# Four groups of instructions moved in the issue order of a fused hybrid decoder layer: sample scores, first query span, first gates, sample softmax

## The chip, the cores and the metric

One Trainium2 chip, one core. The metric is the device time of one execution in microseconds (us). Engines: TensorE (PE; its weight loads are PEld), VectorE (DVE), ScalarE (ACT), GpSimd (POOL), and SyncE (SP), which here issues the DMA transfers. Each engine works through its own queue of instructions in the order in which the program issues them, and waits where an instruction's data or buffer is not ready.

## The reference

One step of a decoder layer (sequence 4096, model width 1024, float32). A combined input projection gives q, k, v, two gates and the LRU input. Half of the heads' width is dilated window attention, the other half a gated linear recurrence; both are gated, concatenated, projected, added to the input and normalised.

```python
def _layer(x_p, x_s, ck, cv, sc, sh, w_in, ...):
    q, k, v, ga, xl, gl = _project(x_p, w_in)
    # 8 heads x 64; patterns (window, dilation) (128,1), (512,4), (2048,16)
    y_att = _merge([_dilated_prompt(qh, kh, vh, d) for _, d in DIL_PATTERNS])
    # causal conv of width 4, then two block-diagonal gates and a linear scan
    h_lru, conv_p, h_p = _lru_branch(xl, 0, 0, conv_w, conv_b, w_ra, b_ra, w_ri, b_ri, lru_lambda)
    y_p = _finish(x_p, y_att, ga, h_lru, gl, w_out, ln_g, ln_b)
    # the same for 8 x 4 sample tokens, against caches of 2048 keys and values
    ...

def _finish(x, y_att, g_att, h_lru, g_lru, w_out, ln_g, ln_b):
    mixed = concatenate([y_att * silu(g_att), h_lru * silu(g_lru)], axis=-1)
    z = ALPHA * x + einsum('bte,ed->btd', mixed, w_out)
    return layer_norm(z) * ln_g + ln_b
```

The prompt is one sequence of 4096 tokens; the sample is 8 sequences of 4 new tokens, each with 2048 cached keys and values. Sample scores are products of the new queries with cached keys, summed over 64 channels.

## The kernel before

Every matrix product is made of three matmuls: each operand is split into a high and a low part, and high x high, high x low and low x high are summed. The order of issue is written out by hand: nothing is reordered behind the program's back, so what the code issues first stands first in its engine's queue.

**Projections (0 to 591 us).** Eight tiles of 512 tokens. For tiles 1 to 6 the program issues four Q groups, four K groups (`qk_group`; 24 matmuls of 128x512 each, L316 to L318) and the value groups (`v_groups`; 96 matmuls, L190). ScalarE and VectorE copy and split each Q or K group (L204, L205), and SyncE stores it (L194). While TensorE works on the values of tile t, `next_chunk` prepares the eight X chunks of tile t+1: VectorE transposes (L111), ScalarE rounds (L114), VectorE takes the difference (L115), SyncE stores a copy for later (L82). `evac_v` then copies four value blocks to tiles `vt` (L210) and stores them (L212). Behind each Q or K group stands one `decode_step`: it issues what the dictionary `decode` holds for that group of the sample scores. A piece is a load of keys (`dec_load`, L366 or L370: 1 MB, or 256 KB for the pattern of dilation 1), a multiply by the queries (`dec_mul`, L375), a sum (`dec_sum`, L380) and a store (`dec_save`, L383). Twelve pieces start at every second group:

```python
g = 2 * n
for d, f in ((0, dec_load), (1, dec_mul), (2, dec_sum), (3, dec_save)):
    decode.setdefault(int(g + d), []).append((f, b, p))
```

Key tiles lie in a pool of two; the small keys lie in the ring of three tiles `vt` that the value copies use too. In the last tile `kp_group` (four transposes, L335, of keys for the output, and their store, L339), `each` (gate weights and the X chunks of a later filler, L123 and L75), `load_K` (L439) and `load_Q` (L446) stand around the groups: attention's first K and the four spans of its first Q.

**Attention (592 to 1457).** Eight units of scores, softmax and values, with projections of the output gate as filler between them (L707 to L712); `vload` loads the values. The first matmul (L562) needs K and the first Q span.

**LRU (1430 to 1900).** 16 tiles of 256 tokens, each in two halves p (called pairs here). Per tile: projection `xl` (`xl_mm`, L140 to L144, 48 matmuls per pair), convolution on VectorE (L958), split of u to `uh` (ScalarE L966, VectorE L967), gates (`gate_mms`, 12 matmuls per pair, L921 to L923; `gate_act`; `gate_vec`), scan, output gate. The order is a list of functions sorted by tick, 18 ticks per tile; `t0` and `t0x` give tile 0 ticks of its own. X chunks come from DRAM (L75); `gated_load`, `gated_mul`, `gated_store` (L1149, L1153, L1157) stand between them.

**Out projection (1888 to 2333).** 32 blocks of 128 tokens (48 matmuls of 128x512, L1341). Per block, VectorE adds the residual (L1395), takes the statistics (L1399, L1401), and scales (L1406, L1408, L1421), and splits the mixed input of a later block (L1330). In between run the remaining sample pieces: multiplies (L1494) and sums (L1498) of keys, two softmax passes `soft1` to `soft6` (mask add L1501, transposes L1507 and L1509, maximum and exponential L1515 to L1519, normalising L1523 to L1526, transposes L1531, copies to `Z` L1536), and sums over values on TensorE (L1551). The order is the dictionary `plan`, sorted by tick; a block is 8 ticks. `soft_at` holds the ticks of the two softmax passes, `v_step` the spacing of the value pieces behind each.

Of the kernel before, what the change touches and what calls it, by code (L numbers as in the profile page):

```python
# [30 lines left out]
class Kern:  # L31
# [125 lines left out]
    def phase1(self, xs_ctx):  # L157
# [9 lines left out]
        n_t = SEQ // 512  # L167
# [216 lines left out]

        for n, (b, p) in enumerate([(b, p) for b in range(self.early) for p in (2, 0, 1)]):
            g = 2 * n
            for d, f in ((0, dec_load), (1, dec_mul), (2, dec_sum), (3, dec_save)):
                decode.setdefault(int(g + d), []).append((f, b, p))
            if p == 2:
                decode.setdefault(g, []).append((row_q, b))  # L390
        order = dec_mul, row_q, dec_sum, dec_save, dec_load
        tick = [0]
# [6 lines left out]
        def qk_groups(t, j, kp, each=None):  # L399
            for m in range(4):  # L400
                qk_group(t, j, m)
                decode_step()
                if kp >= n_t // 2:
                    kp_group(kp, m)
                if each:
                    each()
# [20 lines left out]
        self.KT = self.S[1].rearrange("p (g h n) -> p g h n", g=8, h=2)  # L427
        for g in (0, 2):
            self.load_K(0, g, 2)
        qk_groups(n_t - 1, 0, n_t - 1, each)  # L430
        self.QT = self.S[0].rearrange("p (g h s n) -> p g h s n", g=4, h=2, s=2)
        for nb in range(4):
            self.load_Q(0, 0, nb)
        ctx.close()

    def load_K(self, c, g, n):
# [6 lines left out]
    def load_Q(self, c, st, nb):  # L443
        for p in range(2):
            for h in range(2):
                self.nc.sync.dma_start(  # L446
                    out=self.QT.bitcast(F32)[p * 64:(p + 1) * 64, nb, h],
                    in_=dap(self.qd, (c * 128 + h * 64) * SEQ + st * ST + nb * SPAN,
                            [[SEQ, 64], [DA * SEQ, 2], [1, SPAN]]))


    def phase2(self):
# [19 lines left out]
        KT, QT, Wg, load_K, load_Q = self.KT, self.QT, self.Wg, self.load_K, self.load_Q  # L472
# [329 lines left out]
        def vload(i):  # L802
            x = steps[i]
            if x.b:
                return
            g = x.st * 4 + x.a
            if x.unit.i == 6 and x.a == 0 and x.pat:
                f = (load_V16, load_V4, load_V1)[x.pat]
                f(x.c, g - 1)
                return defer(5, f, x.c, g)  # L810
            if x.pat == 0:
                if x.st:
                    load_V16(x.c, 0, x.a)
                load_V16(x.c, x.st, x.a)
            elif x.pat == 1:
                load_V4(x.c, g)
            else:
                load_V1(x.c, g)

        vload(0)  # L820
        vload(4)
        feed(self.f0[0])
        N, staged, split = len(steps), 0, 0
        for i in range(N + 26):
# [39 lines left out]
            if i < N and x.b == 3 and (x.pat == 1 and x.a or x.pat == 0 and x.a == 3):  # L864
                nb = x.a if x.pat else 0
# [21 lines left out]
    def phase3(self):  # L887
# [14 lines left out]
        T, n_t = 256, SEQ // 256  # L902
# [320 lines left out]
        for i, (f, g, a) in enumerate(early):  # L1223
            t, b = self.e0 + i // len(self.e1), i % len(self.e1)
# [12 lines left out]
        for t in range(n_t):  # L1237
            for tick, i, f, a in plan:
                if f is x_next and t + 1 == n_t:
                    continue  # L1240
                if t == 0 and f is gl_mm:
                    tick = self.t0[0] + a[0]
                if t == 0 and f is x_next:
                    tick = self.t0x[0] + self.t0x[1] * a[0]
                if t == 0 and a == (1,) and f in (gate_mms, gate_act):
                    tick = self.t0[1 + (f is gate_act)]
                ticks.setdefault(t * period + tick, []).append((i, t, f, a))
        for g in sorted(ticks):
            for i, t, f, a in sorted(ticks[g], key=lambda v: (v[1], v[0])):
# [427 lines left out]
@with_exitstack  # L1677
def tile_hymba_dilated_attn_rglru(ctx, tc, ins, outs):
    k = Kern(ctx, tc, ins, outs)
    k.pr = 0.2, 5.5, 7.0  # L1680
    k.p2 = 6, 9, 5, 1, 1, 3, 4, 3, 7, 11, 12, 16, 20, 24, 24, 24, 24, 17, 381, 387, 3.95
    k.kl, k.lag, k.f0, k.wl, k.fill_rate = k.p2[:7], k.p2[7:13], k.p2[13:18], k.p2[18:20] + (2,), (k.p2[20],) * 8
    k.t0x = 1.5, 1.5, (1,) * 8, (1, 1, 0, 1, 1, 0, 1, 1)
    k.t0 = -9.0, 22.2, 23.0
    k.ev = 0, 1, 0, 0
    k.p4 = 6.55, 12.0, 13.5, 14.1, 18.2, 9.0, 2.0, 6.5
    k.ls = 356, 358, 360, 364, 366, 368, 370, 372, 374, 376
    k.nx = lambda nc, t, c: nc.gpsimd if t == 0 and c % 2 else None
    k.s0 = lambda nc, i: nc.gpsimd if i < 9 and i % 2 else None
    k.soft = 0.49, 2.0, 5.0, 5.5, 9.5, 11.0, 12.75, 4.77, 7.0  # L1690
    k.p3 = 0, 4.0, 3.75, 4.5, 7.4, 8.2, 9.4, 11.8, 12.0, 17.0, 12.2, 13.0, 16.0, 18.5, 25.5, 20.55, 22.2, 28.5, 30.25, 33.0, 31.5, 34.75
    k.svb, k.we, k.wo0, k.wo1, k.wo2 = 4, (lambda nc, j, c: nc.vector), 6.0, 1.4, 4.4
    k.xe, k.le, k.ll = (lambda nc: nc.gpsimd), (lambda nc: nc.gpsimd), 5
    k.e0, k.e1, k.e2, k.smp = 4, (2,), (9,), (5, 14)
    k.early, k.k_start, k.k_step, k.soft_at, k.v_step = 4, 10.0, 22.0, (14.0, 114.0), (24.0, 22.0)
    xs = k.xs_ctx = ExitStack()
    k.phase1(xs)
    k.open_late(xs)
    k.phase2()
    k.phase3()  # L1700
    k.phase4()
    xs.close()
# [28 lines left out]
```

## Time and profile before

| | us |
|---|---|
| median of 3 runs (lowest to highest) | 2335.94 (2334.12 to 2345.07) |
| the profiled execution, its own time | 2335.18 |
| its span | 2333.5 |
| TensorE busy (share of the span) | 2193.2 (94%) |
| VectorE busy | 1424.5 (61%) |
| ScalarE busy | 1093.0 (47%) |
| GpSimd busy | 529.9 (23%) |
| mean granted TensorE clock | 0.97 of full speed |

The span goes from the first to the last instruction; the 1.7 us between it and the time lie around it. The shares are means over stages with different limits. Where an engine stands still, the profile names what ended the wait. The granted clock is given in tenths of full speed; a window that shows 0.50 ran at the lower of two levels.

### The profile page before, as it was taken

The page shows a single profiled execution, that of the slowest core. Times are in us where ns is not written, and L with a number is a line of the kernel's source. Part 1 is how long each engine was busy: PE and PEld are TensorE (multiplying, and loading weights), DVE is VectorE, ACT ScalarE, POOL GpSimd, SP SyncE. Part 2 cuts the span into 40 slices and gives each one's busy share as a digit, 9 for nine tenths or more (in the row PEclk, how much of TensorE's full clock was granted, in tenths as well). Part 3 has the DMA queues.
Part 4 walks back from the last instruction along what each step waited for, and adds up shares of the span by engine and source line. Part 5 has one row for each costly group of instructions (what it writes and reads, how often), then busy time and mean ns, then how long its engine had stood idle before and what let it go on. Part 6 is the DMA issues. An engine that isn't in the chain of part 4 may idle for free.

```text
span 2333.5 us, 42473 instructions
## 1 busy us (share of the span) xinstructions
PE 2193.2 (94%) x15274; PEld 1891.7 (81%) x15274; DVE 1424.5 (61%) x3544; ACT 1093.0 (47%) x2819; POOL 529.9 (23%) x499
## 2 busy tenths in 40 slices
PE   6999999999799989989998997899999988999998
PEld 5887778888688889978988886899999965777776
DVE  4454443332267677766765765677878778865465
ACT  3211112222267657766766673666777742212121
POOL 1000000000247465656837576000000000000000
PEclk9999999999899999999999998999999998999999
DMA  6867666555966888788798665545545656755541
GB/s 176 256 215 224 220 220 211 185 205 187 263 157 165 188 202 190 199 212 199 194 209 204 170 175 125 183 152 167 163 154 181 195 205 239 263 183 191 189 144 59
DMA packets 325058, 444.57 MB, mean 191 GB/s; under 512 B 60405, under 2 KB 195573, under 8 KB 319729
## 3 DMA queue, kind: packets, MB, share of 16 engines
q1 hardware_dynamic: 322128, 432.94, 63.4%
q0 software_dynamic: 2720, 8.92, 1.1%
q8 instruction: 122, 2.00, 0.4%
q14 instruction: 88, 0.71, 0.1%
HBM read 305.99 MB, written 135.80 MB: 189 GB/s over the span
## 4 chain that ended last, share of the span: by engine, by line
PE 69%; DMA 13%; DVE 5%; POOL 5%; SPq 4%; issue 3%; ACT 2%; ACTq 0%; POOLq 0%; DVEq 0%
PE po L1341 15%; PE o L598 6%; PE pp L190 6%; PE pt L582 6%; DMA dk<-in_cache_k_dram 3%; PE s L562 3%; PE s L563 3%; PE pg L1019 2%; PE pg L1021 2%; PE pg L1020 2%; PE pp L316 2%; PE pp L317 2%; PE pp L318 2%; PE xl L144 2%; PE xl L140 2%
## 5 line engine op out<-in xcount | busy, mean ns | idle before, releaser
L512 POOL CAST qg<-S 128x512 fp32r<-128x512 f32 x256 | 277.0, 1105 | 655.7 <-DMA S<-qd 500.0
L1341 PE MATMUL po<-S,mx 128*128 128x512 f32 x1536 | 371.9, 402 | 10.4 <-DVE xr L1395 7.1
L1341 PEld LDWEIGHTS po<-S,mx 128*128 128x128 f32 x1536 | 290.3, 191 | 95.8 <-issue 17.3
L573 ACT ACTIVATE sm<-sm,st 128x256 f32<-128x256 f32 (+1 forms) x512 | 251.8, 493 | 181.9 <-DVE st L569 134.2
L569 DVE CUSTOM_DVE_ANT_0 sm<-s,mask 128x256 f32<-128x256 f32 (+1 forms) x768 | 269.5, 389 | 83.4 <-PE s L563 72.7
L586 DVE COPY pts<-pt 128x512 f32<-128x512 f32 x228 | 157.0, 689 | 147.4 <-PE pt L582 145.1
L582 PE MATMUL pt<-ident,sm 128*128 128x128 f32 x1368 | 227.6, 285 | 0.1
L598 PE MATMUL o<-pts,v 128*64 128x128 f32 x2736 | 197.5, 285 | 6.6 <-DMA v<-vd 5.2
L562 PE MATMUL s<-S,qg 128*128 128x256 f32 x512 | 160.1, 333 | 37.0 <-POOL qg L512 24.5
L190 PE MATMUL pp<-S,xh 128*128 128x512 f32 x768 | 179.2, 393 | 6.5 <-ACT S L128 5.3
L316 PE MATMUL pp<-xh,S 128*128 128x512 f32 x448 | 179.6, 401 | 4.0 <-ACT xh L114 3.5
L582 PEld LDWEIGHTS pt<-ident,sm 128*128 128x128 f32 x1368 | 153.9, 142 | 34.3 <-ACT sm L573 17.2
L317 PE MATMUL pp<-xh,S 128*128 128x512 f32 x448 | 178.7, 399 | 1.7 <-DVE xh L115 1.7
L598 PEld LDWEIGHTS o<-pts,v 128*64 128x64 f32 x2736 | 149.3, 139 | 34.3 <-DMA v<-vd 5.7
L318 PE MATMUL pp<-xh,S 128*128 128x512 f32 x448 | 177.0, 395 | 0.0
L190 PEld LDWEIGHTS pp<-S,xh 128*128 128x128 f32 x768 | 145.5, 190 | 38.6 <-ACT S L128 6.2
L707 PE MATMUL f<-xh,S 128*128 128x256 f32 x512 | 147.8, 289 | 3.4 <-DMA xh<-xtd 3.4
L140 PE MATMUL xl<-xh,S 128*128 128x256 f32 x512 | 146.3, 286 | 4.0 <-DMA xh<-xtd 2.6
L573 ACT ACTIVATE sm<-sm,ac 128x128 f32<-128x128 f32 (+1 forms) x256 | 114.4, 448 | 75.1 <-DVE ac L569 73.5
L205 DVE TENSOR_TENSOR stg<-pp,stg 128x512 fp32r<-128x512 f32 x56 | 50.9, 912 | 159.2 <-ACT stg L204 159.0
L144 PE MATMUL xl<-xh,S 128*128 128x256 f32 x512 | 146.2, 286 | 1.7 <-POOL S L129 0.8
L712 PE MATMUL f<-xh,S 128*128 128x256 f32 x512 | 147.3, 288 | 0.0
(289 smaller groups left out, 5150.9 us busy)
## 6 DMA issues: line engine op xcount, KB each, us to landing
xh<-xtd SPq DMA_DIRECT2D x256, 256.0 KB
S<-qd SPq DMA_DIRECT2D x128, 256.0 KB
xtd<-xh SPq DMA_DIRECT2D x56, 512.0 KB
gb<-wd SPq DMA_DIRECT2D x64, 384.0 KB
v<-vd SPq DMA_DIRECT2D x264, 64.0 KB
S<-kd SPq DMA_DIRECT2D x64, 256.0 KB
xr<-in_x_prompt_dram SPq DMA_DIRECT2D x32, 512.0 KB
arena<-in_cache_v_dram SPq DMA_DIRECT2D x16, 1024.0 KB
```

What stands on the lines that cost most here:

```text
L140: nc.tensor.matmul(out, wh, xh, start=(c == 0), stop=False)
L190: nc.tensor.matmul(p, l, m, start=(c == 0 and a + b == 0), stop=(c == 7 and (a, b) == ((1, 0) if j < 2 else (0, 1))))
L316: nc.tensor.matmul(ps, wh, xh, start=(c == 0), stop=False)
L317: nc.tensor.matmul(ps, wh, xl, start=False, stop=False)
L318: nc.tensor.matmul(ps, wl, xh, start=False, stop=(c == 7))
L512: nc.gpsimd.tensor_copy(o, q.bitcast(F32))
L562: nc.tensor.matmul(s[:, h], q_ap(x, h, 0), k, start=True, stop=False)
L569: nc.vector.tensor_tensor_reduce(x.sm[:, h, o], s[:, h, i], self.mask[:, x.pat, o], -0.125, 3e38, ALU.add, ALU.min, x.stat[:, h, 0:1])
L573: nc.scalar.activation(x.sm[:, h, o], x.sm[:, h, o], AF.Exp, bias=x.stat[:, h, 0:1], scale=-1.0, accum_out=x.stat[:, h, 1:2])
L582: nc.tensor.transpose(p[:, h, kb], x.sm[:, h, kb * 128:(kb + 1) * 128], self.ident)
L598: nc.tensor.matmul(o[h * 64:(h + 1) * 64, x.b * 128:(x.b + 1) * 128], v[:, h * 64:(h + 1) * 64], x.pt[:, h, kb], start=(kb == kbs[0]), sto ...
L1341: self.nc.tensor.matmul(ps[j], l, self.Wo[j][c][:, s], start=(c == 0 and s == 0 and l is mh), stop=(c == 7 and l is ml))
```

## The change

Four edits, all to the order of issue; no instruction is added or removed. Sample pieces in the projections: multiply, sum and store come one group later than before, two, three and four groups behind the load. The last tile's loop is written out, so that the first Q span's load is issued right behind the store of the last Q group, and the other three spans between the two value loads of attention. Tile 0's gates get ticks of their own for both pairs. The first softmax pass moves from tick 14 to 26, the second from 114 to 116, with 22 ticks between value pieces in the first pass in place of 24.

```diff
@@ -384,7 +384,7 @@
 
         for n, (b, p) in enumerate([(b, p) for b in range(self.early) for p in (2, 0, 1)]):
             g = 2 * n
-            for d, f in ((0, dec_load), (1, dec_mul), (2, dec_sum), (3, dec_save)):
+            for d, f in ((0, dec_load), (2, dec_mul), (3, dec_sum), (4, dec_save)):
                 decode.setdefault(int(g + d), []).append((f, b, p))
             if p == 2:
                 decode.setdefault(g, []).append((row_q, b))
@@ -427,10 +427,13 @@
         self.KT = self.S[1].rearrange("p (g h n) -> p g h n", g=8, h=2)
         for g in (0, 2):
             self.load_K(0, g, 2)
-        qk_groups(n_t - 1, 0, n_t - 1, each)
         self.QT = self.S[0].rearrange("p (g h s n) -> p g h s n", g=4, h=2, s=2)
-        for nb in range(4):
-            self.load_Q(0, 0, nb)
+        for m in range(4):
+            qk_group(n_t - 1, 0, m)
+            if m == 3:
+                self.load_Q(0, 0, 0)
+            kp_group(n_t - 1, m)
+            each()
         ctx.close()
 
     def load_K(self, c, g, n):
@@ -818,6 +821,8 @@
                 load_V1(x.c, g)
 
         vload(0)
+        for nb in range(1, 4):
+            load_Q(0, 0, nb)
         vload(4)
         feed(self.f0[0])
         N, staged, split = len(steps), 0, 0
@@ -1242,8 +1247,8 @@
                     tick = self.t0[0] + a[0]
                 if t == 0 and f is x_next:
                     tick = self.t0x[0] + self.t0x[1] * a[0]
-                if t == 0 and a == (1,) and f in (gate_mms, gate_act):
-                    tick = self.t0[1 + (f is gate_act)]
+                if t == 0 and f in (gate_mms, gate_act, gate_vec):
+                    tick = self.t0[1 + a[0]][(gate_mms, gate_act, gate_vec).index(f)]
                 ticks.setdefault(t * period + tick, []).append((i, t, f, a))
         for g in sorted(ticks):
             for i, t, f, a in sorted(ticks[g], key=lambda v: (v[1], v[0])):
@@ -1681,7 +1686,7 @@
     k.p2 = 6, 9, 5, 1, 1, 3, 4, 3, 7, 11, 12, 16, 20, 24, 24, 24, 24, 17, 381, 387, 3.95
     k.kl, k.lag, k.f0, k.wl, k.fill_rate = k.p2[:7], k.p2[7:13], k.p2[13:18], k.p2[18:20] + (2,), (k.p2[20],) * 8
     k.t0x = 1.5, 1.5, (1,) * 8, (1, 1, 0, 1, 1, 0, 1, 1)
-    k.t0 = -9.0, 22.2, 23.0
+    k.t0 = -9.0, (18.5, 18.6, 19.5), (24.5, 24.6, 25.5)
     k.ev = 0, 1, 0, 0
     k.p4 = 6.55, 12.0, 13.5, 14.1, 18.2, 9.0, 2.0, 6.5
     k.ls = 356, 358, 360, 364, 366, 368, 370, 372, 374, 376
@@ -1692,7 +1697,7 @@
     k.svb, k.we, k.wo0, k.wo1, k.wo2 = 4, (lambda nc, j, c: nc.vector), 6.0, 1.4, 4.4
     k.xe, k.le, k.ll = (lambda nc: nc.gpsimd), (lambda nc: nc.gpsimd), 5
     k.e0, k.e1, k.e2, k.smp = 4, (2,), (9,), (5, 14)
-    k.early, k.k_start, k.k_step, k.soft_at, k.v_step = 4, 10.0, 22.0, (14.0, 114.0), (24.0, 22.0)
+    k.early, k.k_start, k.k_step, k.soft_at, k.v_step = 4, 10.0, 22.0, (26.0, 116.0), (22.0, 22.0)
     xs = k.xs_ctx = ExitStack()
     k.phase1(xs)
     k.open_late(xs)
```

VectorE at the boundary between tiles 1 and 2, where the cutting of tile 2's X begins (L111, L115), as a piece of the difference (`dk` are key tiles, `stg` a copied Q or K group, `sc` scores, `vt` values):

```order
 L205 TENSOR_TENSOR stg<-pp,stg 128x32x16
 L380 TENSOR_REDUCE sc<-dk 128x32
-L205 TENSOR_TENSOR stg<-pp,stg 128x32x16
-L375 TENSOR_TENSOR dk<-dk_1302,qb 128x2048
 L111 STREAM_TRANSPOSE raw<-X 128x512
 L115 TENSOR_TENSOR xh<-raw,xh 128x2x256
```

```order
 L115 TENSOR_TENSOR xh<-raw,xh 128x2x256
 L210 COPY vt<-pp 128x512 x2
+L205 TENSOR_TENSOR stg<-pp,stg 128x512
+L375 TENSOR_TENSOR dk<-dk_1300,qb 128x2048
 L205 TENSOR_TENSOR stg<-pp,stg 128x512
 L380 TENSOR_REDUCE sc<-dk 128x32
```

The last multiply that stood ahead of the cutting now stands behind the copies of the values and one Q group; a sum stands ahead of the cutting. The other two such boundaries change alike.

TensorE at the start of the LRU stage, before: the last projection of tile 0 (`xl_16493`), the gates of tile 0, pair 0 (`z`), the first projection of tile 1 (`xl_16615`):

```order
L144 MATMUL xl_16493<-xh_15946,S2_79 128x256
L921 MATMUL z_16584<-uh_16555,S0_77 128x256
...
L923 MATMUL z_16591<-uh_16555,S0_77 128x256
L140 MATMUL xl_16615<-xh_16485,S2_79 128x256
L142 MATMUL xl_16615<-xh_16485,S2_79 128x256
```

The same place in the changed kernel; the first projection of tile 1 is `xl_16586` there, its second `xl_16686`:

```order
L144 MATMUL xl_16493<-xh_15946,S2_79 128x256
L140 MATMUL xl_16586<-xh_16485,S2_79 128x256
...
L144 MATMUL xl_16586<-xh_16582,S2_79 128x256
L926 MATMUL z_16639<-uh_16555,S0_77 128x256
...
L928 MATMUL z_16646<-uh_16555,S0_77 128x256
L140 MATMUL xl_16686<-xh_16485,S2_79 128x256
```

The 12 gate matmuls moved behind the 48 projection matmuls. Those of pair 1 keep their place.

VectorE in the out projection, before: from the mask add (L1501) to the softmax (L1516 on) stand the residual sum of block 1 and what belongs to it (`xr`, `bs`, `mv`: residual, statistics; `mx`: the split mixed input; `SC`, `arena`: sample scores and keys):

```order
L1421 TENSOR_TENSOR xr<-xr,lnb 128x1024
L1501 TENSOR_TENSOR SC_22083<-SC_22083,m_22121 128x128
L1395 SCALAR_TENSOR_TENSOR xr<-xr,po 128x512 x2
L1399 BN_STATS bs<-xr 128x6 x2
L1401 BN_AGGR mv<-bs 128x2
L1498 TENSOR_REDUCE SC_22083<-arena 128x32
L1330 SCALAR_TENSOR_TENSOR mx<-A,mx 128x256 x4
L1494 TENSOR_TENSOR arena<-arena,qb 128x2048
L1516 TENSOR_TENSOR dP<-ds,mn 128x32
```

The changed kernel: the mask add is L1506, the softmax L1521 on, the residual sums L1400:

```order
L1335 SCALAR_TENSOR_TENSOR mx<-B,mx 128x256 x4
L1506 TENSOR_TENSOR SC_22083<-SC_22083,m_22121 128x128
L1411 RECIPROCAL mv<-mv 128x1
L1413 SCALAR_TENSOR_TENSOR xr<-xr,mv,lng 128x1024
L1426 TENSOR_TENSOR xr<-xr,lnb 128x1024
L1400 SCALAR_TENSOR_TENSOR xr<-xr,po 128x512 x2
L1404 BN_STATS bs<-xr 128x6 x2
L1406 BN_AGGR mv<-bs 128x2
L1521 TENSOR_TENSOR dP<-ds,mn 128x32
```

The mask add now stands behind the residual sum of block 2, three key sums and two mix splits further down. On TensorE block 3 has come ahead of the score transposes, and block 4 ahead of the softmax's transposes.

## Rows read from the trace of the kernel before

A row of a stretch gives its limits, its length, the busy us and (x) instructions of PE, PEld, DVE, ACT and POOL, the granted clock, the mean busy share of the DMA engines and GB/s.

**Rows 1.** the page's shares: each engine's busy us, share of the span, instructions.

```profile
PE 2193.2 (94%) x15274; PEld 1891.7 (81%) x15274; DVE 1424.5 (61%) x3544; ACT 1093.0 (47%) x2819; POOL 529.9 (23%) x499
```

**Rows 2.** chain of waits, value groups of tiles 4 and 5: start us, us, engine, output, line.

```profile
366.86 21.76 PE pp L190 x96
434.04 21.76 PE pp L190 x96
```

**Rows 3.** timeline of TensorE, projections: start us, us, engine, line, operation, output<-input, count.

```profile
154.83 18.75 PE L190 MATMUL pp<-S,xh 128*128 128x512 f32 x82
...
227.72 13.99 PE L190 MATMUL pp<-S,xh 128*128 128x512 f32 x61
...
299.76 16.48 PE L190 MATMUL pp<-S,xh 128*128 128x512 f32 x72
...
567.84 0.60 PE L335 MATMUL pp<-ident,kf 128*128 128x128 f32 x4
568.19 0.48 PE L316 MATMUL pp<-xh,S 128*128 128x512 f32 x1
```

**Rows 4.** timeline of VectorE, projections [idle before <-releaser]; then groups, 150 to 345 us.

```profile
164.51 0.70 DVE L111 STREAM_TRANSPOSE raw<-X 128x512 f32<-128x512 f32 x1
...
235.19 2.29 DVE L375 TENSOR_TENSOR dk<-dk,qb 128x2048 f32<-128x2048 f32 x1 [3.41 <-DMA dk<-in_cache_k_dram]
...
310.48 0.70 DVE L111 STREAM_TRANSPOSE raw<-X 128x512 f32<-128x512 f32 x1
...
369.12 0.70 DVE L111 STREAM_TRANSPOSE raw<-X 128x512 f32<-128x512 f32 x1
...
L380 DVE TENSOR_REDUCE sc<-dk 128x32 f32<-128x2048 f32 x10 | 22.8, 2280 | 0.0
```

**Rows 5.** timeline of ScalarE behind the value groups of tile 1.

```profile
196.49 0.59 ACT L210 COPY vt<-pp 128x512 f32<-128x512 f32 x1 [15.66 <-DMA vd<-vt]
```

**Rows 6.** timeline of TensorE, start of attention; then one stretch of all engines.

```profile
606.30 0.55 PE L562 MATMUL s<-S,S 128*128 128x256 f32 x1 [11.31 <-DMA S<-qd]
625.58 0.35 PE L707 MATMUL f<-xh,S 128*128 128x256 f32 x1 [3.35 <-DMA xh<-xtd]
...
605.00:610.00 5.00, 3.40 (x14) 3.17 (x15) 0.51 (x4) 0.88 (x4) 2.27 (x3) 0.50 1.07 226
```

**Rows 7.** timeline of TensorE at the start of the LRU stage, and a stretch behind it.

```profile
1462.48 0.58 PE L922 MATMUL z<-uh,S 128*128 128x256 f32 x1 [5.75 <-DVE uh L967]
1471.21 0.38 PE L140 MATMUL xl<-xh,S 128*128 128x256 f32 x1 [0.29 <-DMA xh<-xtd]
...
1480.00:1875.00 395.00, 395.00 (x3237) 388.90 (x3237) 306.08 (x604) 291.33 (x540) 0.00 (x0) 1.00 0.52 164
```

**Rows 8.** timeline of TensorE in the out projection, blocks 2 to 4.

```profile
1909.79 13.03 PE L1341 MATMUL po<-S,mx 128*128 128x512 f32 x48 [6.57 <-DVE xr L1395]
...
1935.93 0.87 PE L1531 MATMUL dt<-ident,dP 128*128 128x128 f32 x3 [11.71 <-DVE dP L1526]
...
1936.66 13.16 PE L1341 MATMUL po<-S,mx 128*128 128x512 f32 x48
...
1951.70 11.51 PE L1341 MATMUL po<-S,mx 128*128 128x512 f32 x48
```

**Rows 9.** timeline of VectorE in the out projection.

```profile
1922.93 1.28 DVE L1395 SCALAR_TENSOR_TENSOR xr<-xr,po 128x512 f32<-128x512 f32 x2
...
1931.26 0.18 DVE L1516 TENSOR_TENSOR dP<-ds,mn 128x32 f32<-128x32 f32 x1
...
1935.70 0.16 DVE L1406 RECIPROCAL mv<-mv 128x1 f32<-128x1 f32 x1
...
1944.15 2.26 DVE L1498 TENSOR_REDUCE SC<-arena 128x32 f32<-128x2048 f32 x1
...
1947.68 0.14 DVE L1406 RECIPROCAL mv<-mv 128x1 f32<-128x1 f32 x1
```

**Rows 10.** a stretch of the out projection, columns as in the window of rows 6.

```profile
1910.00:1950.00 40.00, 28.25 (x115) 22.09 (x119) 35.63 (x61) 11.39 (x22) 0.00 (x0) 0.79 0.76 279
```

## Prediction

> **What bounds the kernel now.** I read the shares of the engines first: TensorE is busy 94% of the span [rows 1], so the time is TensorE's work plus the stretches in which it stands still or runs slowly. Then I read where it stands still near what the change moves, stage by stage.
>
> In the projections, the four value groups of a tile are 96 matmuls and 21.76 us when nothing stops them [rows 2], 0.2267 us each, so the 288 matmuls of a tile cost at least 65.3 us. The value groups of tiles 1, 2 and 3 end at 173.58, 241.71 and 316.24 (start plus duration) [rows 3], those of tiles 4 and 5 at 388.62 and 455.80 [rows 2]. From end to end the tiles 2 to 5 last 68.1, 74.5, 72.4 and 67.2 us. Tile 5 also holds four groups of four transposes, each 0.35 us from its first to what follows [rows 3], so an undisturbed tile is 67.2 - 1.4 = 65.8. Tiles 2, 3 and 4 lose 2.3, 8.7 and 6.6 us, together 17.6. (Against 65.3 it is 19.1, against 67.2 it is 13.4: the bounds.)
>
> VectorE shows the cause. It must cut and split a tile's X while TensorE works on the values of the tile before. In front of that stands a multiply of a sample piece that waits for its keys: 3.41 us, then 2.29 us of work, to about 237.4 [rows 4]. Counted from the start of the value groups (their end less 21.76: 151.8, 219.9, 294.5) the cutting begins 12.7, 17.5 and 16.0 us late (164.51, 237.4, 310.48), and the tile behind loses 2.3, 8.7 and 6.6. Per us of lateness that is 1.3 us, and nothing is lost up to some 11 us. Tile 4, which has no sample piece there, begins at 369.12 [rows 4], 2.3 us late, and tile 5 loses nothing.
>
> At the hand-over to attention TensorE waits 11.31 us for the Q load and later 3.35 us for an X chunk, while the DMA engines are full (share 1.07, 226 GB/s) and the granted clock is 0.50 [rows 6]. At the start of the LRU stage it waits for the first converted u (last step 5.75 us), and then for X chunks to 1471.21; from 1480 to 1875 it never stops [rows 7]. In the out projection it waits 6.57 us on the first residual sum and 11.71 us on the softmax [rows 8].
>
> **The change part by part**, against the profiled execution, 2335.18 us.
>
> *Sample pieces.* The same loads, multiplies and sums are issued, multiply and sum one group later. At these three boundaries a sum then stands ahead of the cutting, not the multiply that waits. Its operand was multiplied two groups' evacuations before, so it waits for nothing and takes 2.28 us [rows 4]. It follows the last K evacuation, as the cutting in tile 4 does at +2.3, so cutting begins at about 2.3 + 2.2 = +4.5 us, 6.5 us inside the 11 that cost nothing. The displaced multiply now runs behind the value evacuation, where VectorE has nothing else. A load that is still waited for 3.41 us after one group of 5.44 needs some 9 us; two groups give it 10.9. Two prices remain. A small key tile is held for one group longer, in the ring of three that the value copies also use; already ScalarE waits 15.66 us there for a value store to land [rows 5], and it costs TensorE nothing as long as free PSUM banks last (four groups of 5.44 us). And any multiply may still be late for its load, where only sample work stands behind it. I take the whole 17.6 less 0.6 for these: **-17.0**. Bounds: -18, when even the half-clock tail goes, and -12, which is the low loss of 13.4 less 1.4 for one delayed group.
>
> *Q span.* Two 256 KB transfers (a k_prompt store and an X chunk) no longer stand ahead of the first Q span: 0.5 MB at 226 GB/s is 2.2 us, that much earlier could the 11.31 us wait end. But the DMA engines are full, the bytes ahead of the X chunk that is waited for next, at 625.58, are unchanged, and what attention gains before that is lost to a longer wait there. I take **-0.5**; bounds -2.2 and +1 (the first values come behind one Q span, and three spans behind them).
>
> *First gates.* Only the 12 gate matmuls of tile 0, pair 0 change their place on TensorE; pair 1 keeps its own although its numbers are new, and no other engine's order changes. Before, they ran behind the wait for u and ahead of tile 1's first projection, which then waited for X chunks to 1471.21. Now that projection starts at once and waits for the same chunks, which land no earlier: they are queued behind transfers that wait on GpSimd's and the gates' data, not on TensorE. So the projection ends where it did, and the gates, which were covered by its waits, come behind: 12 x 0.122 (395.00 / 3237) = **+1.5**. Behind it TensorE is full to 1875, so it passes through to the end. Bounds: 0, when the chunks come earlier, and +4, when the projection also runs longer at the half clock (12 of its matmuls cost 0.21 there for 0.12).
>
> *Softmax.* All its steps stay and move 12 ticks (the second set 2). Before, the mask add stood just ahead of the residual sums at 1922.93, TensorE did the score transposes, and block 3 waited 11.71 us for VectorE's 4.4 us of softmax (1931.26 to 1935.70) behind six other pieces of work [rows 8, 9]. Now block 3 goes first: it may start at about 1924 (behind two residual sums) and end near 1935.5 (11.5 us). But the mask add has moved behind norms, sums, mix split and multiply of block 1 and 2. VectorE does from 1922.93 to 1947.68 all of that plus the softmax, 4.44, and the weight copies, 1.2 [rows 9]: 24.75 - 5.6 = 19.1 us. The mask add so comes at about 1942 (1922.93 + 19.1), TensorE waits 6.6 us there, block 4 runs from 1943.6 to about 1956.5 with its start at the half clock (48 matmuls took 13.03 and 13.16 behind waits, 11.51 without [rows 8]), and behind it the order puts a norm's end, a residual sum with its statistics, the softmax, two multiplies, a mix split and a scaling, 18.7 us by the same steps, ahead of the weight copies' end, near 1960.7, so the first value matmuls wait 3 us more. Block 5 then starts near 1962.7, or 1964.1 with a second start at the half clock; before, it started at 1964.2 (1951.70 + 11.51, and 8 value matmuls). VectorE is busy 35.63 of 40 us there [rows 10]: the order says who waits, not how much work stands in front. I take **0**; bounds -13 (the wait of 11.71 and its 1.5 us at the half clock really go) and +5 (two more waits, each with such a tail).
>
> TensorE's clock speaks against this part. Behind waits of 6.57 and 11.71 us the rows show 1.5 and 1.7 us more for 48 matmuls. The Trainium skill (TensorE: Matmul & The Clock Gate, section "HAM oscillation — how this bites in real kernels") says that a loop that pauses for data in each pass goes back to the half clock again and again and pays for the return each time. By that, three waits in place of two would cost one return more and the sum would be -14.5; whether a wait of 3 us does it, no row of this stage shows.
>
> Sum: -17.0 - 0.5 + 1.5 + 0 = **-16.0**, 2319.2, rounded to 2319.5. The profiled execution stands 0.8 us under the median of the runs shown (2335.94), so no correction is made. A measurement of this kernel can tell about 0.5%, 11.7 us, from no change: faster means below 2324.3.
>
> **The rivals.**
> - *The softmax wait goes too.* For it: block 3 no longer stands behind the softmax, and VectorE has idle time (4.4 us in 40). Against it: the 19.1 us of work in front. If VectorE gets through it by the end of block 3, about 12 us more are won: 2307.5.
> - *The tile waits go only in part.* For it: the multiply two places ahead of the cutting still waits for keys, and a load of 9 us has under 2 us to spare. If loads take some 20 us now, that multiply, the last copies and the sum come late together and cutting begins at some +13.7; by 1.3 us per us behind +11 each boundary keeps 3.5 us, the tiles gain 7 instead of 17, and with +1 from the rest the time is 2329. It decides from 6.5 us of lateness on.
> - *Slower: the value copies block.* One ring of three tiles serves small key tiles and value copies. With a key tile held across the value evacuation, both copying engines wait for a store to land. The groups behind then fill the PSUM banks, four at the first boundary and five at the others (21.8 and 27.2 us). Stores now let ScalarE go at 196.49, 22.9 us after the value groups end. If they land 33 us after that end, TensorE waits 33 - 21.8 = 11.2 and twice 5.8, 22.8 us, and the time is 2319.2 + 22.8 = 2342. It decides from about 22 us on at the first boundary; I expect VectorE's release near 13 us, when the first of the four stores has landed.
> - *The move does nothing.* Excluded for part 1, whose order differs at all three boundaries; it is so for pair 1 of the gates, and that is in the sum.
>
> **How the numbers follow.** Forecast 0.62, with its own range 2313 to 2327 from the bounds of its terms (-12 to -18 for the tiles, -2.2 to +4 beside them). Softmax gained 0.14; tile waits in part 0.16; slower 0.04; 0.04 spread over other mishaps on both sides. The range takes in the first two rivals' centres and leaves out the slower one and the tails: 2307 to 2330. Faster by over 0.5%: 0.14 and nearly all of 0.62 (0.56), 0.70; within 0.5%: the rest of the forecast, the third case and half of the spread, 0.26; slower 0.04.
>
> **What would show it.** In the projections: tiles 2 to 4 of 66 to 67 us and cutting that begins under 7 us behind the first value matmul. Wrong, if a multiply with a wait for keys still stands there, or TensorE waits on ScalarE's or VectorE's copies at the groups behind. At the hand-over: attention's first matmul 1 to 2 us earlier, its X chunk wait longer. In the LRU: no wait on u ahead of tile 1's projection, gates some 1.5 us later than without the move, the last X chunk at the same distance. In the out projection: the wait of 11.71 gone, and one of 5 to 8 us on the mask add and one of 2 to 4 us on the weight copies in its place. The forecast falls if the three tiles still last over 70 us, or if block 5 of the out projection moves by over 4 us relative to block 2.

## The result, and the profile after

The changed kernel takes 2321.55 us, median of 7 runs (2318.08 to 2326.34), against 2335.94 (2332.86 to 2345.07, 7 runs). The ratio is 0.993, 95% interval 0.9911 to 0.995: some 0.7% faster (0.6% by the two medians). The forecast was 2319.5, range 2307 to 2330. The profiled execution took 2319.85 us with a span of 2318.1, 15.4 us less than the span before.

The page's shares of the changed kernel, which answer to [rows 1]:

```profile
PE 2182.0 (94%) x15274; PEld 1890.0 (82%) x15274; DVE 1425.0 (61%) x3544; ACT 1092.8 (47%) x2819; POOL 529.6 (23%) x499
```

No work went away. TensorE's busy time fell by 11.2 us, mostly because matmuls that ran between waits, in part at the lower clock, now run back to back at the higher one. Its idle time fell by 4.2 us.

The value groups in TensorE's timeline, tiles 1 to 3 of the changed kernel, against [rows 3]:

```profile
152.34 21.92 PE L190 MATMUL pp<-S,xh 128*128 128x512 f32 x96
...
217.62 21.92 PE L190 MATMUL pp<-S,xh 128*128 128x512 f32 x96
...
282.90 21.92 PE L190 MATMUL pp<-S,xh 128*128 128x512 f32 x96
```

They stand exactly 65.28 us apart: 288 x 0.2267, a tile with no stop in it. (The duration counts the last matmul to its end; the next work starts 21.76 us after the first.) Before, TensorE stopped there for the X that was cut late. These are all its waits from 150 to 460 us (total us, times, longest), and one stretch in which it ran at the lower clock; the changed kernel has no wait in that window:

```profile
PE pp L316 <- ACT xh L114: 3.5, 6, 0.6
PE pp L317 <- DVE xh L115: 1.7, 8, 0.2
247.50:257.50 10.00, 9.52 (x18) 5.19 (x18) 5.38 (x9) 2.34 (x4) 0.00 (x0) 0.50 0.61 232
```

The waits add up to 5.2 us, against 19.2 us that tiles 2 to 4 lost. In the stretch shown TensorE did 18 matmuls, 4.1 us of work at 0.2267 each, in 10 us: 5.9 of the 9.3 us that tile 3 lost lie there. VectorE's timeline of the changed kernel, against [rows 4]: the multiply, the sum and the first cut at the end of tile 2, the first cut at the end of tile 3.

```profile
215.25 2.29 DVE L375 TENSOR_TENSOR dk<-dk,qb 128x2048 f32<-128x2048 f32 x1 [0.59 <-DMA dk<-in_cache_k_dram]
...
220.02 2.27 DVE L380 TENSOR_REDUCE sc<-dk 128x32 f32<-128x2048 f32 x1
222.22 0.69 DVE L111 STREAM_TRANSPOSE raw<-X 128x512 f32<-128x512 f32 x1
...
287.49 0.70 DVE L111 STREAM_TRANSPOSE raw<-X 128x512 f32<-128x512 f32 x1
```

The cutting begins 4.6 us after the first value matmul (222.22 against 217.62), 17.6 before. The multiply that still stands two places ahead waits 0.59 us for its keys, and the cutting is not late by it.

The hand-over and the start of the LRU stage in TensorE's timeline, and one stretch, against [rows 6, 7]:

```profile
588.06 0.55 PE L565 MATMUL s<-S,S 128*128 128x256 f32 x1 [11.55 <-DMA S<-qd]
...
608.19 0.55 PE L710 MATMUL f<-xh,S 128*128 128x256 f32 x1 [4.78 <-DMA xh<-xtd]
```

```profile
1442.58 0.55 PE L140 MATMUL xl<-xh,S 128*128 128x256 f32 x1 [13.69 <-DMA xh<-xtd]
...
1450.31 0.58 PE L140 MATMUL xl<-xh,S 128*128 128x256 f32 x1 [3.24 <-DMA xh<-xtd]
...
1456.66 0.28 PE L926 MATMUL z<-uh,S 128*128 128x256 f32 x1
...
1450.00:1455.00 5.00, 4.69 (x22) 4.70 (x23) 0.00 (x0) 0.00 (x0) 0.00 (x0) 0.50 0.61 189
```

The wait on u is gone from TensorE; a wait of 13.69 us on the first X chunk stands in its place, and the projection behind it runs at 0.50 of the clock.

The out projection in TensorE's timeline, blocks 2 to 5, against [rows 8]:

```profile
1893.51 12.97 PE L1346 MATMUL po<-S,mx 128*128 128x512 f32 x48 [6.73 <-DVE xr L1400]
1906.91 11.86 PE L1346 MATMUL po<-S,mx 128*128 128x512 f32 x48 [0.43 <-DVE xr L1400]
...
1925.54 0.47 PE L1512 MATMUL ds<-ident,SC 128*128 128x128 f32 x1 [6.56 <-DVE SC L1506]
...
1927.38 13.03 PE L1346 MATMUL po<-S,mx 128*128 128x512 f32 x48
...
1945.41 1.89 PE L1556 MATMUL do<-vs,Z 32*8 32x512 f32 x8 [4.57 <-DVE Z L1542]
...
1949.05 12.51 PE L1346 MATMUL po<-S,mx 128*128 128x512 f32 x48
```

The 11.71 us have become 6.56 on the mask add and 4.57 on the weight copies.

Where the 15.4 us of span went, from the times at which the same work starts in both traces:

| stretch | before, us | after, us | difference |
|---|---|---|---|
| start to the end of the last value group | 544.61 | 526.13 | -18.5 |
| to attention's first matmul | 61.69 | 61.93 | +0.2 |
| to the end of tile 0's last LRU projection | 842.31 | 840.83 | -1.5 |
| to the gates of tile 0, pair 1 | 31.70 | 34.97 | +3.3 |
| to block 2 of the out projection | 429.48 | 429.65 | +0.2 |
| to block 5 | 54.33 | 55.54 | +1.2 |
| to the end | 369.38 | 369.05 | -0.3 |

### The profile page after: what moved, and what is told of

Its sections match the earlier page's. It is cut to its first block, busy times and chain, and to the rows that moved or that the text cites. A ratio compares the mean times of both kernels' runs of the same rounds, so it can differ in the third digit from the quotient of the medians.

```text
span 2318.1 us, 42476 instructions
## 1 busy us (share of the span) xinstructions
PE 2182.0 (94%) x15274; PEld 1890.0 (82%) x15274; DVE 1425.0 (61%) x3544; ACT 1092.8 (47%) x2819; POOL 529.6 (23%) x499
## 4 chain that ended last, share of the span: by engine, by line
PE 48%; DMA 6%; POOL 4%; DVE 4%; issue 2%; ACT 1%; SPq 1%; POOLq 0%; ACTq 0%; DVEq 0%
PE po L1346 14%; PE pt L585 4%; PE o L601 4%; PE pg L1024 2%; PE xl L140 2%; PE pg L1026 2%; PE pg L1025 2%; PE xl L144 2%; PE xl L142 2%; PE s L565 2%; PE s L566 2%; DMA gb<-wd 2%; POOL u L860 2%; POOL qg L515 2%; PE do L1556 1%
## 5 line engine op out<-in xcount | busy, mean ns | idle before, releaser
L316 PE MATMUL pp<-xh,S 128*128 128x512 f32 x448 | 175.9, 393 | 0.0
L318 PE MATMUL pp<-xh,S 128*128 128x512 f32 x448 | 174.6, 390 | 0.0
L317 PE MATMUL pp<-xh,S 128*128 128x512 f32 x448 | 174.4, 389 | 0.0
```

The lines of the kernel that those rows point to most:

```text
L316: nc.tensor.matmul(ps, wh, xh, start=(c == 0), stop=False)
L318: nc.tensor.matmul(ps, wl, xh, start=False, stop=(c == 7))
```

## The experiments

**Each edit alone.** The diffs are the four parts of the change, each applied to the kernel before without the others. The tiles:

```diff
-            for d, f in ((0, dec_load), (1, dec_mul), (2, dec_sum), (3, dec_save)):
+            for d, f in ((0, dec_load), (2, dec_mul), (3, dec_sum), (4, dec_save)):
```

> The sample pieces alone are moved; the rest is as before. Theory (the cutting of X began late): tiles 2 to 4 last 65.3 to 66 us each, and the time is 17 to 19 us under before, since the stage then carries the whole gain and the other three edits cancel or cost. Rival (the gain came partly from the other edits): the tiles give 12 us or less, about 2324.

2316.33 us, ratio 0.9924 (0.9902 to 0.9947), 18.8 us under the 2335.11 of before. Tiles 2 to 4 last 65.28 us each. The theory holds: this edit alone carries the gain, and the whole change, at a ratio of 0.993, shows no more.

The first query span:

```diff
+            if m == 3:
+                self.load_Q(0, 0, 0)
...
         vload(0)
+        for nb in range(1, 4):
+            load_Q(0, 0, nb)
```

> The first query span alone is moved ahead. Theory (the transfers are the bound there, and the first span lands no earlier): the wait ahead of attention's first matmul stays within 1 us of 11.3, the X chunk wait behind it grows by 1 to 1.5 us, and the time is within 2 us of before. Rival (part of the gain of the whole change is from here): attention begins 2 us earlier against the last value group and the time is 2 us or more under before.

2334.31 us, ratio 0.9997 (0.9983 to 1.001). Attention's first matmul in its TensorE timeline, and the wait for the X chunk behind it:

```profile
605.80 0.55 PE L565 MATMUL s<-S,S 128*128 128x256 f32 x1 [10.16 <-DMA S<-qd]
...
626.01 0.55 PE L710 MATMUL f<-xh,S 128*128 128x256 f32 x1 [5.00 <-DMA xh<-xtd]
```

From the end of the value groups to the first matmul 60.5 us (605.80 - 545.26), 61.7 before: 1.2 us sooner, and the wait is 1.15 us shorter, a little more than the 1 us allowed. The X chunk wait grew by 1.6 us, and its end lies 80.75 us behind the value groups, 80.97 before. In this execution the first span came sooner, and the wait behind it took that back. That the edit brings it sooner is not shown: the eleven executions with the old loads lie between 61.3 and 62.7 us, and the whole change, which has this edit too, at 61.9.

The first gates:

```diff
-                if t == 0 and a == (1,) and f in (gate_mms, gate_act):
-                    tick = self.t0[1 + (f is gate_act)]
+                if t == 0 and f in (gate_mms, gate_act, gate_vec):
+                    tick = self.t0[1 + a[0]][(gate_mms, gate_act, gate_vec).index(f)]
...
```

> The first gates alone are moved. Theory (the projection that now stands ahead waits for the same X chunks, and the gates come behind it, at the lower clock for part): the gates of pair 1 of tile 0 start 3 us later against the end of the last projection of tile 0, and the time is 3 us over before. Rival (the 3 us seen at this stage are scatter): within 1 us of before at that place.

2334.06 us, ratio 0.9993 (0.9977 to 1.0009). In the total nothing is seen: the interval is 3.7 us to both sides, and the 3 us over before that were expected lie outside it. In the stage something is: the gates of pair 1 start 37.0 us after tile 0's last projection, and 35.0 in the whole change, against 31.2 to 34.1 in the seven executions that keep the old order and the old loads there (before 31.70; tiles alone 31.29, query span 31.28, softmax 31.17; the three runs below on the lateness 33.78, 33.56 and 34.06). In these executions the edit costs 1 to 6 us there.

The softmax:

```diff
-    k.early, k.k_start, k.k_step, k.soft_at, k.v_step = 4, 10.0, 22.0, (14.0, 114.0), (24.0, 22.0)
+    k.early, k.k_start, k.k_step, k.soft_at, k.v_step = 4, 10.0, 22.0, (26.0, 116.0), (22.0, 22.0)
```

> The softmax move alone. Theory (the wait of 11.7 us is replaced by waits on the mask add and on the weight copies): 6.5 us and 4.5 us of waits on these, block 5 of the out projection 1 us later against block 2, the time 0 to 2 us over before. Rival (the softmax wait goes): 5 us or more under before.

2333.52 us, ratio 0.9992 (0.9978 to 1.0007). Its waits in TensorE's timeline:

```profile
1933.75 0.47 PE L1507 MATMUL ds<-ident,SC 128*128 128x128 f32 x1 [6.56 <-DVE SC L1501]
...
1953.62 1.89 PE L1551 MATMUL do<-vs,Z 32*8 32x512 f32 x8 [4.26 <-DVE Z L1537]
```

From block 2 to block 5 it takes 55.56 us, 55.54 in the whole change, 54.33 before and 53.5 to 54.9 in all eleven executions with the old softmax. The wait did not go, it was divided. The rival's 5 us of gain lie at the edge of the interval, and the stage excludes them.

**Is it the lateness of the cutting, and of three multiplies alone?** Only the three pieces whose multiply stood ahead of the cutting move:

```diff
+            late = g + 1 in (7, 15, 23)
-            for d, f in ((0, dec_load), (1, dec_mul), (2, dec_sum), (3, dec_save)):
+            for d, f in ((0, dec_load), (1 + late, dec_mul), (2 + late, dec_sum), (3 + late, dec_save)):
```

> As before, but the three pieces whose multiply stands ahead of the cutting of X (one at the end of tiles 1, 2 and 3) are moved one group later, and the other nine stay. Theory (only these three multiplies matter, since they make the cutting late): tiles 2 to 4 last 65.3 us as with all twelve moved, the time 17 to 19 us under before. Rival (the gain comes from all twelve key loads having longer to land, or from stores and loads spread otherwise): at most 3 in 12 of it, about 5 us, and tiles still over 68 us.

2321.77 us, ratio 0.9952 (0.9933 to 0.997): 11 us, between the two. Tiles 2 to 4 last 66.3, 70.1 and 67.1. VectorE's timeline at the end of tile 2 shows what theory and rival both left out:

```profile
213.92 2.29 DVE L375 TENSOR_TENSOR dk<-dk,qb 128x2048 f32<-128x2048 f32 x1 [4.67 <-DMA dk<-in_cache_k_dram]
...
224.80 2.29 DVE L375 TENSOR_TENSOR dk<-dk,qb 128x2048 f32<-128x2048 f32 x1 [4.38 <-DMA dk<-in_cache_k_dram]
...
231.26 0.72 DVE L111 STREAM_TRANSPOSE raw<-X 128x512 f32<-128x512 f32 x1
```

The multiply one place further up, which stayed where it was, waits 4.38 us, and everything behind it in the queue, the last two K copies, a sum and the cutting, comes late. The cutting starts 7.7, 12.7 and 11.8 us late, counted from the end of the value groups less their 21.92 us. The copies' lateness itself held PSUM banks, as the first row of TensorE's waits from 150 to 460 us shows (total us, times, longest):

```profile
PE pp L190 <- DVE stg L205: 2.3, 2, 1.5
```

The value groups of tiles 2 and 3 last 22.99 and 23.76 us there for 21.92: these stops are all of the 1.1 us that tile 2 lost and 1.8 of the 4.8 of tile 3. Moving only the multiplies next to the cutting was not enough; which of the other nine had to move was not tried.

**How much lateness costs.** On the tile edit alone, the sum ahead of the cutting is done three or five times more, into a tile that nobody reads:

```diff
+            if tick[0] in (7, 15, 23):
+                x = dqp.tile([128, NS], F32, tag="sx", name="sx", bufs=1)
+                for _ in range(3):
+                    nc.vector.tensor_reduce(x, o.rearrange("p t (h d) -> p (t h) d", d=HD), op=ALU.add, axis=AX.X)
```

> All twelve pieces moved (the tile edit alone), and the sum ahead of the cutting is done three times more at the three boundaries, 3 x 2.2 us of VectorE, into a tile that nobody reads. Cutting then begins at about +11.1 us. Theory (nothing is lost up to some 11 us): tiles 2 to 4 last 65.3 to 66 us. Rival (every us of lateness costs): 6.6 us or more for each tile, 72 us.

> The same with the sum done five times more, so that cutting begins at about +15.5 us, with no wait for keys in front. Theory (1.3 us per us of lateness behind 11): tiles 2 to 4 last some 71 to 72 us, as before the change. Rival (the loss came from the key loads' traffic and not from lateness): 65.3 to 66 us.

One execution each, 2319.92 and 2346.28 us. Tiles 2 to 4 last 66.8, 71.7 and 68.0 with three sums, 72.1, 76.7 and 75.1 with five. At the end of tiles 2 and 3 the cutting came later than planned, since a multiply ahead of it waited longer for its keys; that the longer hold of a key tile delays the next load would explain it, but was not tried. At the end of tile 1 no multiply waited. VectorE's timeline with five sums, end of tile 1 and end of tile 2:

```profile
148.61 2.28 DVE L375 TENSOR_TENSOR dk<-dk,qb 128x2048 f32<-128x2048 f32 x1
...
156.24 11.56 DVE L384 TENSOR_REDUCE sx<-dk 128x32 f32<-128x2048 f32 x5
167.72 0.70 DVE L111 STREAM_TRANSPOSE raw<-X 128x512 f32<-128x512 f32 x1
```

```profile
225.77 2.29 DVE L375 TENSOR_TENSOR dk<-dk,qb 128x2048 f32<-128x2048 f32 x1 [2.47 <-DMA dk<-in_cache_k_dram]
...
231.21 11.58 DVE L384 TENSOR_REDUCE sx<-dk 128x32 f32<-128x2048 f32 x5
242.70 0.70 DVE L111 STREAM_TRANSPOSE raw<-X 128x512 f32<-128x512 f32 x1
```

So the expected lengths of 65.3 to 66 and of 71 to 72 were missed, but lateness and loss go together as forecast. Lateness is the first cut less (end of the value groups - 21.92), 0.16 more than by the prediction's count; loss is the next tile's length less 65.28:

| execution | late, us | loss of the next tile, us |
|---|---|---|
| all twelve moved (whole change; tile edit) | 4.6, 4.6, 4.6 | 0.0, 0.0, 0.0 |
| three moved | 7.7, 12.7, 11.8 | 1.1, 4.8, 1.8 |
| three sums more | 11.4, 14.5, 12.9 | 1.5, 6.5, 2.7 |
| before | 12.9, 17.6, 16.2 | 2.9, 9.3, 7.1 |
| five sums more | 16.1, 19.0, 17.7 | 6.8, 11.5, 9.9 |

A straight line through the points beyond 11 us (these, and three executions more with the old order) rises 1.26 us per us from 10.2 us on, and leaves 0.6 us of scatter (1.6 at most). The line describes, it is no mechanism: it adds the waits for X and the stretches at the lower clock. Behind tile 1, before, the granted clock stayed at 1.00 (173.50 to 241.50) and the loss is 2.9; behind tiles 2 and 3 it fell to 0.50 (247.50 to 257.50, shown above, and 322.50 to 329.00), and the losses are 9.3 and 7.1. Lateness makes the loss with or without a wait for keys ahead of the cutting: with five sums, at the end of tile 1, sums alone made 16.1 us of lateness, and 6.8 us were lost. The same key loads cost nothing where the cutting came at +4.6, so their traffic alone does not make the loss.

**What the gates edit lacked.** The projection that it puts ahead had no X, because a gated load (L1154 in the changed kernel) that waits for GpSimd stands before the X chunks in SyncE's queue. SyncE's timeline of the changed kernel, and that wait (total us, times, longest):

```profile
1422.64 1.23 SPq L660 DMA_DIRECT2D gb<-wd  x2
1436.25 0.38 SPq L1154 DMA_DIRECT2D pa<-ad  x1
...
1437.19 2.09 SPq L75 DMA_DIRECT2D xh<-xtd  x4
...
SPq L1154 <- POOL u L860: 7.5, 1, 7.5
```

On the tile and gates edits:

```diff
+                if t == 0 and f is gated_load and a == (0,):
+                    tick = 4.32
                 if t == 0 and f is x_next:
-                    tick = self.t0x[0] + self.t0x[1] * a[0]
+                    tick = self.t0x[0] + self.t0x[1] * a[0] if a[0] < 2 else 4.05 + 0.05 * a[0]
```

> The tile edit and the gates edit, and at the start of the LRU stage the six X chunks of tile 1 that have a free buffer are loaded ahead of the first gated load, which waits for GpSimd. Theory (the gates edit cost time because the projection that it puts ahead had no X): that projection begins 10 us sooner, the gates of pair 1 of tile 0 start 23 to 27 us after tile 0's last projection in place of 31.4 (before) and 35 to 37 (gates edit alone), and the time is 4 to 8 us under the tile edit alone, about 2308 to 2312. Rival (the LRU stage is bound there by VectorE and ScalarE, not by X): 30 us or more at that place, and no gain.

2309.22 us, ratio 0.9888 (0.9865 to 0.9911). SyncE's and TensorE's timelines:

```profile
1422.79 4.67 SPq L75 DMA_DIRECT2D xh<-xtd  x6
1434.87 0.37 SPq L1149 DMA_DIRECT2D pa<-ad  x1
...
1438.79 0.81 SPq L75 DMA_DIRECT2D xh<-xtd  x2
```

```profile
1441.81 0.58 PE L140 MATMUL xl<-xh,S 128*128 128x256 f32 x1 [9.59 <-DMA xh<-xtd]
...
1454.93 0.28 PE L921 MATMUL z<-uh,S 128*128 128x256 f32 x1
```

Six chunks are issued 12 us ahead of the gated load. The projection starts at once and then waits 9.59 us for the seventh, which is issued behind that gated load and held 2.9 us more by a store of GpSimd's last result (`ad<-u`) that has to land first. The gates of pair 1 start 26.7 us after tile 0's last projection, as expected.

The same early chunks, the gates where they were before:

> The tile edit and the early X chunks, but the gates of tile 0 where they stood before, ahead of tile 1's first projection. Theory (early X and the gates edit need each other: with the gates in front, TensorE waits for the first split u, some 13 us behind tile 0's last projection, whatever X does): the gates of pair 1 start 27 to 29 us after tile 0's last projection, 1 to 3 us later than the 26.7 of the run with the gates edit. Rival (the X chunks alone are what counts): the same 26.7 us or less.

2313.44 us, ratio 0.9902 (0.9884 to 0.992). The gates of pair 1 start 28.0 us after the last projection, behind a wait of 11.26 us on the split u. That lies 3 to 6 us under the 31.2 to 34.1 of the old order, and comes with X alone. The 1.2 us between these two executions are what was expected of the gates edit with X at hand, but less than the 2.9 us by which seven executions of one order differ at this place: that it gains there is not shown. The totals do not tell these two runs apart either.

All eight chunks early, on the run with six; the last two take buffers that tile 0 has left, and four chunks of tile 2 are loaded later:

```diff
-            XT.setdefault(t + 1, {})[c] = self.x_chunk(t + 1, c, xp2 if c > 5 else None)
+            XT.setdefault(t + 1, {})[c] = self.x_chunk(t + 1, c, xp2 if c > 5 and t else None)
...
-                    tick = 4.32
+                    tick = 4.9
+                if t == 1 and f is x_next and 1 < a[0] < 6:
+                    tick = 6.2 + a[0]
```

> The tile edit, the gates edit and all eight X chunks of tile 1 ahead of the first gated load; the last two come from the ring that tile 0 has left, not from the pool whose memory waits for GpSimd's last stores, and four chunks of tile 2 are loaded later instead. Theory (the 9.6 us wait for the seventh chunk was what was left): that wait goes, TensorE waits for the first split u instead (about 12 us behind tile 0's last projection), and the gates of pair 1 start 20 to 23 us after it in place of 26.7; the time is 3 to 6 us under the run with six early chunks, 2303 to 2306. Rival (tile 2's chunks then come late and give it back): a wait for X ahead of tile 2's first projection and no gain.

2303.83 us (2300.64 to 2305.67), ratio 0.9858 (0.9844 to 0.9873): the lowest median of this study, 32 us under before. TensorE's waits behind tile 0's last projection are these two:

```profile
1426.89 0.36 PE L140 MATMUL xl<-xh,S 128*128 128x256 f32 x1 [1.52 <-DMA xh<-xtd]
...
1439.43 0.58 PE L922 MATMUL z<-uh,S 128*128 128x256 f32 x1 [3.94 <-DVE uh L967]
```

The gates of pair 1 start 23.8 us after the last projection, 0.8 us outside the 20 to 23 expected, and no wait for tile 2's X appears.

Tile 1's second projection, too, ahead of the first gates:

```diff
+                if t == 1 and f is xl_mm and a == (1,):
+                    tick = 1.0
-    k.t0 = -9.0, (18.5, 18.6, 19.5), (24.5, 24.6, 25.5)
+    k.t0 = -9.0, (19.2, 19.3, 20.2), (24.5, 24.6, 25.5)
```

> As the run with all eight chunks early, and tile 1's second projection, too, ahead of the first gates, so that both fill the wait for the first split u. Theory (this wait is filled by work that is ready): the gates of pair 1 start 17 to 20 us after tile 0's last projection, 2 to 4 us less than with one projection ahead. Rival (the second projection needs the PSUM bank that ScalarE frees only behind that same split): no difference, or a start later by up to 2 us.

2307.87 us, ratio 0.9883 (0.9856 to 0.991). Pair 1's gates start 16.8 us after the last projection, even sooner than expected, but TensorE then waits 3.99 us on VectorE ahead of the next output gate (L1019), and the first gates of tile 1 start 30.4 us after it, 31.0 without the edit. What is won ahead is gone by the first gates of tile 1, in part to that wait. The totals of the two runs overlap, so which is faster is open.

## Why the prediction was right

**The tiles**: forecast -17.0 with bounds -12 and -18, measured -18.5 over the stage in the profiled pair (-19.2 over tiles 2 to 4; the execution started 0.7 us late) and 18.8 in time for the edit alone. The cause was named right, and so was the order: a sum of 2.2 us ahead of the cutting, which begins at +4.6 where +4.5 was worked out. (It is +4.4 by the prediction's own count.) The terms that were mis-sized are the length of an undisturbed tile and the two prices. The prediction took 1.4 us of transposes off tile 5 to get 65.8 us; tile 5 lasts 67.2 in the changed kernel too, so its transposes cost 1.9, and the count of matmuls, 65.28, was the right measure: 1.6 us more over three tiles. The 0.6 us of prices were nothing: TensorE has no wait from 150 to 460 us. The sketch "1.3 us per us beyond some 11" came out as 1.26 beyond 10.2, but it leaves out that much of this loss lies in stretches at the lower clock.

**The query span**: forecast -0.5, measured +0.2 at the first matmul of the changed kernel and 1.2 us sooner in the edit alone, gone at the X chunk. The step that the X chunk takes back what the first span gains held in the edit alone; in the changed kernel there was no gain to take back, and the X chunk's wait ended 1.1 us later against the value groups than before (82.06 and 80.97).

**The gates**: forecast +1.5, measured +3.3. The step "12 x 0.122" is the term that was too small. From the last wait for X to the gates of pair 1 it took 9.10 us before (1471.21 to 1480.31) and 13.55 after (1450.31 to 1463.86): 4.45 more, of which 1.4 are the gates, 0.4 three matmuls more (that wait is now on the seventh chunk, before on the eighth) and 2.6 the lower clock, at 0.50 (22 matmuls in 4.69 us, 0.213 each for 0.122). That wait ended 1.2 us sooner. I had the lower clock in the bound of +4 and left it out of the term. The order before had most of its matmuls at the lower clock ahead of its last waits, where they cost nothing. Nor did the projection start at once, as the prediction has it: its first chunk let it go 13.69 us after tile 0's last projection.

**The softmax**: forecast 0, measured +1.2 from block 2 to block 5 and -0.3 behind it. The wait on the mask add was worked out as 6.6 and is 6.56; the one on the weight copies as 3 and is 4.57. Block 4 took 13.03 us, block 5 12.51 and the 16 value matmuls between them 3.6 in place of 1.9, where an undisturbed block takes 11.5: the return to the higher clock was paid behind both waits. The granted clock behind each:

```profile
1927.00:1930.00 3.00, 3.00 (x9) 2.50 (x10) 2.04 (x3) 0.93 (x1) 0.00 (x0) 0.50 1.03 366
1945.00:1951.00 6.00, 5.59 (x21) 1.80 (x22) 5.97 (x9) 1.52 (x5) 0.00 (x0) 0.50 0.26 104
```

The Trainium skill (TensorE: Matmul & The Clock Gate, section "HAM oscillation — how this bites in real kernels") says of a loop that pauses for data in each pass that it pays for the return each time. The rows agree: behind the wait of 4.57 us the return was paid again. The prediction had weighed this return as 1.5 us and left it out of the sum.

**Attention**, which no step touched, took 1.5 us less. Over the runs of this study it lasted 833 to 843 us from its first matmul to the end of tile 0's last projection, so that is scatter. The errors, -1.5 in the tiles, +0.7 at the query span, +1.8 in the gates and +0.9 in the softmax, and this scatter nearly cancel; that the forecast of 2319.5 stands so near 2321.55 is luck, since its terms are worse than that. In the prediction's chances, its own parts give 0.24 and not 0.26 for the case within 0.5%; nothing hangs on it.

**The rivals**: the softmax wait did not go, tile waits did not stay, and the value copies did not block TensorE although ScalarE waited longer than before (its row behind tile 1's values, against [rows 5]):

```profile
190.34 0.59 ACT L210 COPY vt<-pp 128x512 f32<-128x512 f32 x1 [16.82 <-DMA vd<-vt]
```

That is 16.1 us after the value groups end (190.34 - 174.26), inside the 22 us from which it would have decided.

## What to carry to other kernels

In an engine's queue an instruction that waits delays everything behind it, and what that costs is read from the lateness of the work that another engine waits for: here nothing at 4.6 us, 1.5 us at 11.4, and from there on more than a us for each us, clock included. Put a distance between a load and its first use that covers the load's time not only for the pair that stands in front of the critical work: three moved gave 11 us, all twelve 19. And before work is put ahead to fill a wait, look whether its own inputs can be there: in the whole change the gates came 3 us later; with the X chunks moved ahead of a transfer that waits, the same place was reached 5 to 8 us sooner than before the change.

## What was not expected of the hardware

The attention stage, issued alike in these kernels, lasted from 833.0 us (597.71 to 1430.71, the run with three more sums) to 842.8 (586.59 to 1429.38, the tile edit alone) in single executions. So an edit worth 1 to 3 us cannot be seen in the total, whose intervals are 3 to 4 us wide to each side with 10 runs. It can be looked for in its own stage, from one piece of work to the next, beside the scatter of that place: none in the tiles without a stop (65.28 us in every one), 1.4 us around blocks 2 to 5, 2.9 us at the first gates.
